# Stick-breaking attention by parts: the scan sums weights, the values become differences, gated outputs wait in DRAM

## The chip, the cores and the metric

The kernel runs on one core of one Trainium2 chip. The metric is the device time of one execution in microseconds. Kernels are compared by runs on the same chip. A profile of one execution, with a trace of every instruction, stands beside the times.

The engines in the profile are TensorE (PE; its weight loads are PEld), VectorE (DVE), ScalarE (ACT), GpSimd (POOL) and SyncE (SP), which issues the DMAs.

## The reference

Two layers, 1024 tokens, width 1024. Each layer projects the normalised input once, runs four groups of heads beside one another, normalises and gates each group's output, and projects back:

```
h = rmsnorm(x, g_pre) @ w_in
A: sliding-window attention   B: short gated convolution
C: latent attention           D: stick-breaking attention
y = concat(rmsnorm(out_g)) * silu(gate)
x = x + rmsnorm(y @ w_out, g_post)
```

The change is in group D (4 heads of 64):

```
z = q @ k.T * scale                       # per block of 128 queries, strictly causal
log_keep = where(mask, log_sigmoid(-z), 0)
after = cumsum(log_keep, reverse=True) - log_keep
a = where(mask, exp(log_sigmoid(z) + after), 0)
out = a @ v
```

So the weight of key j is its break probability times the product of the keep probabilities of all later keys.

## The kernel before, in words

All matrix products are done in three terms of a high and a low part (`split`: ScalarE casts the high part, VectorE subtracts it to get the low one), so TensorE has much work, and every operand passes ScalarE and VectorE once.

**Streams and planner.** The program is written as streams (Python generators): `gemm` (projections), `scores`, `pvs` (products with the values), `norms`, `z_parts` (splitting the gated outputs for the last projection), `w_out_rows`, `outs`, weight loading and others. `Weaver.run` steps through them and always takes the first stream in its list whose next piece is ready by its own clock; `gemm` is last in the list, so it fills TensorE where the others wait. `Weaver.enter` books each instruction on its engine with a cost from a formula, `Weaver.dma` books each transfer at 355 GB/s with fixed latencies around it (0.7 and 0.6 us ahead of the data, about 0.9 us behind it, 1.22 us from a ScalarE result to the issue), and the order that comes of these bookings is the order that each engine gets. On the chip an engine works through its list in that order and waits where something is late. All DMAs are issued by SP, in order.

**Tiles.** Most results live in 34 tiles `g` of 4 KB per partition: 16 hold the transposed input, 8 the outputs `y` of the four groups (two halves Q of 512 tokens), the others queries, keys, values and weights. Weight matrices `P` of the attention rows have 6 tiles. Projections write to 2 banks (`w_bank`), scores to 3, transposes to 2, value products to 1.

**Group D.** `d_v` projects the values of one tile of 128 tokens at a time (24 matmuls of 256 columns), and ScalarE and VectorE split the bank straight into the value tiles `Vt`. `d_q` and `d_k` project queries and keys of a pair of heads. `d_scores` computes the scores of one head and two blocks of 128 queries, ScalarE makes two sigmoids, the keep probabilities `kt` and the break probabilities `bt`. VectorE multiplies `kt` up from the right with one scan and then multiplies `bt` with the shifted result. `pv_causal` transposes the result on TensorE, splits it, and multiplies it with `Vt`.

**Order of a layer.** Group C's columns, group B, then `d_v`, `d_q(0)`, `d_k(0)`, gate 2, `d_q(1)`, half of gate 1, `d_k(1)` once the scores of the first pair are done, the other half of gate 1, the projections of group A, gate 3, gate 0. Group B's output lies in DRAM (`yBd`) from its normalisation until just before its gate.

Of the kernel before, what the change touches and what calls it, by code (L numbers as in the profile page):

```python
# [12 lines left out]
F32 = mybir.dt.float32  # L13
# [8 lines left out]
P = 128  # L22
S = 1024
D = 1024
# [69 lines left out]
class Weaver:  # L94
# [7 lines left out]
    def __init__(self, tc):  # L102
        self.tc = tc
        self.now = 0.0
        self.busy = {k: [] for k in "AVGDH"}
        self.acc = {}
        self.touched = {}
        self.opened = {}
        self.slots = {}
        self.banks = set()  # L110
        self.read = {}
        self.table = None
        self.users = []
        self.load_at = 0.0
        self.start = 0.0
        self.gone = set()
        self.last, self.tag = {}, {}
        self.funcs = [(0.0, 0)]
        self.port = {"V": [], "G": []}
        self.done = set()  # L120

    def alloc(self, ap, tag, bufs):
# [43 lines left out]
    def after(self, key, a, kinds):  # L166

        p0, p1, lo, hi = self.area(a)
        name = a.tensor.name
        t = self.opened.get(name, 0.0)  # L170
        if name not in self.acc:
            t = max(t, self.last.get(self.tag.get(name), 0.0))
        for (q0, q1, l, h, kind, k), end in self.acc.get(name, {}).items():
            if kind in kinds and q0 < p1 and p0 < q1 and l < hi and lo < h:
                t = max(t, end + LAT.get(k + key, 0.0))
        return t

    def ready(self, key, aps):
        return max([self.after(key, a, "w") for a in aps], default=0.0)
# [68 lines left out]
    def enter(self, key, op, args, kw):  # L248
        aps = [a for a in list(args) + list(kw.values()) if isinstance(a, bass.AP)]
        out = aps[0]  # L250
        outs = [out]
        if "accum_out" in kw:
            outs.append(kw["accum_out"])
        if op == "tensor_tensor_reduce":
            outs.append(aps[-1])
        n = 1
        for d in (aps[1] if op == "tensor_reduce" else out).shape[1:]:
            n *= d
        t = max(self.ready(key, aps[1:]), max(self.after(key, a, "rw") for a in outs))
        read = [a.tensor.name for a in aps[1:] if a.tensor.name in self.banks]  # L260
        bank = bool(read)
        for nm in read:
            for k, end in self.read.get(nm, {}).items():
                t = max(t, end + (LAT[k + key] if k != key else 0.0))
        scalars = sum(
            isinstance(args[i], bass.AP) for i in SCALARS.get(op, ()) if i < len(args)
        )
        func = args[2] if op == "activation" else None
        pair = False
        half = out.shape[0] <= 64 and n >= 128  # L270
        if key == "A":
            dur = (52.0 if bank else 93.0) + 0.833 * n
            dur += 93.5 * sum(isinstance(kw.get(k), bass.AP) for k in ("scale", "bias", "accum_out"))
            dur += 125.0 * half
            if func in TABLES and func:
                t = max(t, self.load_at)
        elif key == "V":
            fast = op == "tensor_scalar" and not bank
            dur = 69.0 + (0.52 if fast else 1.04) * n + 62.0 * scalars + 95.0 * half
            pair = (fast or op == "tensor_tensor") and not bank and n >= 128  # L280
            if op == "tensor_tensor_scan":
                dur = 110.0 + 2.12 * n
                pair = True
            elif op == "tensor_reduce":
                dur += 117.0
        elif op == "affine_select":
            dur = 244.0
        elif op == "memset":
            dur = 36.0 + 0.83 * n
        elif op == "tensor_scalar":  # L290
            dur = 244.0 + 0.833 * n
        else:
            dur = 148.0 + 2.25 * n
            pair = n >= 128
            if args[-1] == ALU.pow:
                dur = 400.0 + 162.0 * n
                pair = False
        t = self.place(key, t, dur, pair=pair)
        if key == "A" and func in TABLES and func:
            self.funcs = self.funcs[-60:] + [(t, func)]  # L300
        self.tc.cur_priority = int(t)
        for nm in read:
            self.read.setdefault(nm, {})[key] = t + dur
        by = "S" if op in ("tensor_tensor_scan", "tensor_tensor_reduce") else key
        for a in outs:
            self.note(by, a, "w", t + dur, t)
        for a in aps[1:]:
            self.note(key, a, "r", t + dur)
        return t
# [78 lines left out]
def tile_hybrid_trunk(  # L388
# [317 lines left out]
    def w_tiles():  # L706
# [11 lines left out]
        for L in LS:  # L718
# [11 lines left out]
                    chunk(L, f"B{key}{m}", c0 + m * P, P)  # L730
            chunk(L, "DV", O_DV, 256, True)
            for key in (
                "DQ0", "DK0", "G20", "G21", "DQ1", "G10", "DK1", "G11", "AV0", "AQ0", "AK0", "AQ1",
                "G30", "G31", "G00", "G01",
            ):
                if key[0] == "G":
                    c0 = O_G + 256 * int(key[1])
                else:
                    c0 = dict(DQ=O_DQ, DK=O_DK, AK=O_AK, AV=O_AV, AQ=O_AQ)[key[:2]]
                chunk(L, key, c0 + int(key[2]) * P, P, key == "G01")  # L740
# [412 lines left out]


    def group_b(L):
        l, yd = L["l"], L["yBd"]
        for m in range(2):
            us = [ftile(516), ftile(516)]

# [35 lines left out]
        A.activation(dst, pb, AF.Tanh, scale=0.5)  # L1195
        V.scalar_tensor_tensor(dst, dst, 1.0, pb, ALU.add, ALU.mult)

    def gate(L, grp, ms=(0, 1)):
        def ev(Q, pb):
            t = ftile()  # L1200
            silu(t, pb)
            z = L["y"][grp][Q]
            G.tensor_tensor(z[:, m, :], z[:, m, :], t, ALU.mult)
            W.release(t)

        for m in ms:
            yield from chunk_T(L, f"G{grp}{m}", ev)

    def gate_by_half(L):
# [12 lines left out]


    def d_v(L):
        yield room(4)
        Vt = [[gtile([P, 4, 2, P]) for _ in range(2)] for _ in range(NQ)]
        L["dV"] = Vt
        for t in range(NT):
            pb = w_bank()
            yield from mm3_w(L, "DV", pb[:, 0:256], "r", xtok(L["xt"], t), 2)  # L1230
            src = pb[:, 0:256].rearrange("p (m h d) -> p m h d", m=2, h=2)
            dst = [Vt[t // 4][hp][:, t % 4] for hp in range(2)]
            for hp in range(2):
                A.copy(dst[hp][:, :, 0:64], src[:, hp])
            for hp in range(2):
                V.tensor_tensor(
                    dst[hp][:, :, 64:128], src[:, hp], f(dst[hp][:, :, 0:64]), ALU.subtract
                )
            W.release(pb)
        done_with(L["W", "DV"])  # L1240

    def d_q(L, hp):
# [16 lines left out]
    def d_scores(L, hp, t0, hh):  # L1259
# [3 lines left out]
        for t in (t0, t0 + 1):  # L1263
# [6 lines left out]
            for o in range(0, w, cut):  # L1270
# [8 lines left out]
                A.activation(kt[:, o : o + n], sc[:, :n], AF.Sigmoid, scale=-0.125)  # L1279
                A.activation(bt[:, o : o + n], sc[:, :n], AF.Sigmoid, scale=0.125)  # L1280
                W.release(sc)
            rev = kt[:, w - 1 :: -1]
            V.tensor_tensor_scan(rev, rev, rev, 1.0, ALU.mult, ALU.bypass)
            V.tensor_tensor(bt[:, 0 : w - 1], bt[:, 0 : w - 1], kt[:, 1:w], ALU.mult)
            W.release(kt)
            Ps.append(bt)
        L["tasks"].append(
# [215 lines left out]
    ZORDER = (4, 5, 2, 3, 6, 7, 0, 1)  # L1503

    def z_split(L, grp, Q, wait=True):
        z = L["y"][grp][Q]
        free = W.idle_from("V")
        ts = []
        for m in range(2):
            if wait:  # L1510
                yield lambda: (ts or W.room("g", 2, 34)) and max(0.0, free() - 4000.0)
            ts = ts or [gtile([P, 2, 512]) for _ in range(2)]
            t = ts[m]
            split(t[:, 0, :], t[:, 1, :], z[:, m, :])
# [66 lines left out]
    for l in range(depth):  # L1581
        LS.append(
            dict(
                l=l, w=w_in[l], last=l == depth - 1, tasks=[], y=[[None, None] for _ in range(4)],
                yBd=[dp.tile([P, 2, 512], F32, name=nm("yBd")) for _ in range(NQ)],
                xt=[None, None], zt=[[None] * NK for _ in range(NQ)],
                wo=[[None] * NK for _ in range(2)],
                ss=cp.tile([P, 4 * NT], F32, name=nm("ss")),
# [54 lines left out]
    def gemm():  # L1643
        for L in LS:
# [11 lines left out]
            yield need(("norm", l, 2, 1))  # L1656
            yield from gate(L, 2)
            yield from d_q(L, 1)
            yield need(("norm", l, 1, 1))
            yield from gate(L, 1, (0,))  # L1660
            yield need(("scores", l, "D0"))
            yield from d_k(L, 1)
            W.mark("D", l, 1)
            yield from gate(L, 1, (1,))
            yield from a_v(L)
            yield from a_q(L, 0)
            yield need(("scores", l, "D1"))
            yield from a_k(L)
            yield from a_q(L, 1)
            yield need(("pv", l, "D1", 1))  # L1670
            L["y"][0] = [gtile([P, 2, 512], F32) for _ in range(NQ)]
            W.mark("A", l)
            yield need(("norm", l, 3, 1))
# [123 lines left out]
    def norms():  # L1797
        for L in LS:
            l = L["l"]
            yield need(("B", l))  # L1800
            for Q in range(NQ):
                y = [ftile(), L["yB1"][Q]]
                dma(y[0], L["yBd"][Q][:, 0, :])
                yield W.when(y[0])
                yield from group_norm_cols(l, 1, y)
                for m in range(2):
                    dma(L["yBd"][Q][:, m, :], y[m])
                W.release(*y)
            for Q in range(NQ):
                yield from norm(L, 2, "C", Q)  # L1810
            yield need(("D", l, 0))
            for Q in range(NQ):
                yield room(1)
                L["y"][1][Q] = gtile([P, 2, 512], F32)
                dma(L["y"][1][Q], L["yBd"][Q])
                W.mark("norm", l, 1, Q)
            yield need(("scores", l, "D1"))
            for Q in range(NQ):
# [52 lines left out]
```

## Time and profile before

| | us |
|---|---|
| median of 3 runs (lowest to highest) | 1160.34 (1159.23 to 1161.73) |
| the profiled execution: its time | 1160.64 |
| its span, first to last instruction | 1158.8 |
| TensorE busy | 1133.3 |
| VectorE busy | 815.0 |
| ScalarE busy | 639.7 |
| POOL busy | 345.0 |

The profiled execution's granted TensorE clock is 0.998 of full speed. Line 85 of the kernel is the helper through which all VectorE, ScalarE and POOL instructions go, line 497 is that of the matmuls, line 501 that of the transposes and line 414 that of the DMAs, so instructions are told apart by the tiles that they write and read: `xP` is an attention row, `xsc` a score bank, `xtr` a transpose bank, `xw` a projection bank or a weight tile, `xg` one of the 34 tiles, `xPT` a transposed and split attention row. A group in the profile reads: line, engine, operation, out<-in, shapes, xcount | busy us, mean ns of one | idle us before them and what ended it.

Stages in layer 0: the value projection of group D runs from 197 to 229 us, `d_q(0)` and `d_k(0)` to 251 us, group D's scores and products from 255 to 405 us, group A to about 495 us. Layer 1 has the same stages from 769, 799, 825 and 975 us on.

### The profile page before, as it was taken

Reading aid. Unit: us, or ns where it says so; the run is one execution under the profiler, and the core shown is the slowest. Engines: PE = TensorE matmul, PEld = TensorE weight load, DVE = VectorE, ACT = ScalarE, POOL = GpSimd, SP = SyncE. Lnnn points to the kernel's source line nnn. Section 1 sums busy time; section 2 is a strip of 40 time slices with the busy share of each in tenths; the row PEclk is TensorE's granted clock in tenths of the full one; section 3 lists DMA queues with packets and bytes.
Section 4 is the critical chain, followed back from the end, with each engine's and each line's share of the span. In section 5 each row is a group of like instructions: output and inputs, shape, how many; then the busy total and the mean of one; then the engine's idle time right before and its main releaser. Section 6 shows DMA issues by size and latency. Waiting matters only on the chain. (4 is left out here: it accounts for less than half of the span.)

```text
span 1158.8 us, 17859 instructions
## 1 busy us (share of the span) xinstructions
PE 1133.3 (98%) x6302; PEld 978.0 (84%) x6302; DVE 815.0 (70%) x1682; ACT 639.7 (55%) x1443; POOL 345.0 (30%) x480
## 2 busy tenths in 40 slices
PE   8999999999999999999999999999999999999997
PEld 6988889988888788878889888899888787887886
DVE  6868788549868988842764677874697789887324
ACT  7666566246656667632554655652664566875211
POOL 3215144114324244210231352530342333531000
PEclk9999999999999999999999999999999999999999
DMA  6120312121011012311450121121201101114123
GB/s 224 42 64 29 83 26 58 46 74 37 19 46 28 19 38 72 107 46 62 150 173 20 38 68 42 38 64 38 82 19 38 37 19 37 29 55 164 55 77 123
DMA packets 72677, 71.97 MB, mean 62 GB/s; under 512 B 10062, under 2 KB 59276, under 8 KB 72588
## 3 DMA queue, kind: packets, MB, share of 16 engines
q1 hardware_dynamic: 72588, 70.83, 20.6%
q8 instruction: 50, 0.82, 0.3%
q14 instruction: 39, 0.32, 0.1%
HBM read 55.09 MB, written 11.53 MB: 57 GB/s over the span
## 5 line engine op out<-in xcount | busy, mean ns | idle before, releaser
L497 PE MATMUL xw<-xg,xw 128*128 128x512 f32 x2064 | 516.8, 396 | 3.5 <-DVE xf L85 2.7
L497 PEld LDWEIGHTS xw<-xg,xw 128*128 128x128 f32 x2064 | 376.4, 188 | 78.1 <-DVE xf L85 4.4
L497 PE MATMUL xsc<-xg,xg 128*128 128x512 f32 (+7 forms) x1400 | 304.4, 363 | 0.4 <-DVE xs L85 0.4
L497 PEld LDWEIGHTS xsc<-xg,xg 128*128 128x128 f32 (+1 forms) x1400 | 238.9, 190 | 35.4 <-DVE xs L85 1.6
L85 POOL TENSOR_SCALAR xP<-xP,xs 128x256 f32<-128x256 f32 (+7 forms) x128 | 81.9, 652 | 169.7 <-DVE xs L85 77.7
L85 ACT CAST xPT<-xtr 128x512 fp32r<-128x512 f32 (+1 forms) x192 | 100.5, 553 | 56.4 <-PE xtr L501 54.9
L501 PE MATMUL xtr<-ident,xP 128*128 128x128 f32 (+1 forms) x843 | 122.5, 273 | 5.6 <-DVE xP L85 4.9
L85 DVE TENSOR_TENSOR xPT<-xtr,xPT 128x512 fp32r<-128x512 f32 (+1 forms) x192 | 116.3, 629 | 13.1 <-ACT xPT L85 12.6
L497 PE MATMUL xw<-xg,xg 128*128 128x416 f32 (+2 forms) x648 | 116.8, 327 | 0.2 <-DVE xg L85 0.2
L497 PE MATMUL xpv<-xPT,xg 128*128 128x256 f32 (+1 forms) x720 | 114.9, 286 | 0.4 <-DVE xPT L85 0.3
L497 PEld LDWEIGHTS xpv<-xPT,xg 128*128 128x128 f32 x720 | 102.9, 189 | 10.6 <-DVE xPT L85 1.9
L501 PEld LDWEIGHTS xtr<-ident,xP 128*128 128x128 f32 (+1 forms) x843 | 97.4, 140 | 16.0 <-DVE xP L85 6.7
L85 POOL TENSOR_TENSOR xw<-xraw,xw 128x512 fp32r<-128x512 f32 x47 | 68.4, 1458 | 138.9 <-ACT xw L85 106.5
L85 DVE TENSOR_TENSOR xg<-xw,xg 64x512 fp32r<-64x512 f32 (+1 forms) x112 | 62.8, 573 | 62.4 <-ACT xg L85 61.2
L85 ACT CAST xg<-xw 64x512 fp32r<-64x512 f32 (+1 forms) x112 | 53.6, 493 | 93.2 <-PE xw L497 81.6
L85 ACT ACTIVATE xP<-xP,xs 128x256 f32<-128x256 f32 (+7 forms) x128 | 80.7, 631 | 43.7 <-DVE xs L85 40.3
L497 PEld LDWEIGHTS xw<-xg,xg 128*128 128x128 f32 x648 | 102.1, 189 | 2.7 <-DVE xg L85 0.4
L85 DVE TENSOR_TENSOR_SCAN xP<-xP 128x128 f32<-128x128 f32 (+3 forms) x64 | 90.5, 1414 | 3.0 <-ACT xP L85 2.7
L85 POOL TENSOR_TENSOR xt<-xt 64x128 f32<-64x128 f32 x64 | 41.6, 650 | 146.5 <-DVE xt L85 131.6
L85 ACT ACTIVATE xP<-xsc 128x512 f32<-128x512 f32 (+2 forms) x192 | 79.7, 514 | 6.6 <-DVE xP L85 6.0
L85 ACT ACTIVATE xt<-xsc 128x512 f32<-128x512 f32 x32 | 19.1, 598 | 113.2 <-PE xsc L497 89.3
L85 ACT COPY xt<-xpv 64x512 f32<-64x512 f32 x80 | 46.7, 584 | 53.5 <-PE xpv L497 52.4
(129 smaller groups left out, 1284.5 us busy)
## 6 DMA issues: line engine op xcount, KB each, us to landing
xraw<-in_w_in_dram SPq DMA_DIRECT2D x96, 256.0 KB, 2.8
xP<-in_w_out_dram SPq DMA_DIRECT2D x16, 512.0 KB, 4.3
xg<-in_x_dram SPq DMA_DIRECT2D x8, 512.0 KB, 8.6
xg<-xP SPq DMA_DIRECT2D x32, 128.0 KB, 2.4
xP<-in_x_dram SPq DMA_DIRECT2D x8, 512.0 KB, 4.1
xP<-xs SPq DMA_DIRECT2D x8, 512.0 KB, 3.8
xs<-xP SPq DMA_DIRECT2D x7, 512.0 KB, 3.6
out_dram<-xP SPq DMA_DIRECT2D x7, 512.0 KB, 2.6
```

The lines of the kernel that those rows point to most:

```text
L85: ins = real(*args, **kw)
L497: in_order(T.matmul(ps, lhs, rhs, start=start, stop=stop, skip_group_check=True))
L501: in_order(T.transpose(ps, src, idn))
```

## The change

The weight of key j is the difference of two neighbouring values of a running sum: with S_j = kt_j * S_(j+1) + bt_j from the right, the weight of key j is S_j - S_(j+1), and summing by parts gives out = sum of S_j * (v_j - v_(j-1)). So `d_scores` leaves S from one scan, without the multiplication behind it, and `d_v` makes differences of neighbouring tokens' values. Tokens lie on partitions, so the value of the token before is one partition away; `differ` fetches it by DMA within SBUF, once for each half of 512 tokens.

Beside it: the outputs of groups 1 (B) and 2 (C) are written to DRAM after their gates and read back in `z_split`; `d_k(1)` comes ahead of gate 1 and no longer waits for the scores of the first pair; the output tiles of group A wait for room instead of the end of group D's products; and the planner's cost formulas are changed (`held`: a longer time where an operand starts in another group of 32 partitions than that of the instruction before; more operations count as using the port that VectorE and POOL share).

```diff
     def enter(...):
-        half = out.shape[0] <= 64 and n >= 128
+        half = self.held(key, out, aps[1:])
...
-            pair = (fast or op == "tensor_tensor") and not bank and n >= 128
+            pair = not bank and n >= 128 and op != "memset"
...
         elif op == "tensor_scalar":
             dur = 244.0 + 0.833 * n
+            pair = n >= 128
...
-    def gate(L, grp, ms=(0, 1)):
+    def gate(L, grp):
...
             G.tensor_tensor(z[:, m, :], z[:, m, :], t, ALU.mult)
             W.release(t)
+            if m and grp in L["yd"]:
+                dma(L["yd"][grp][Q], z)
+                W.release(z)
...
     def d_v(L):
         yield room(4)
         Vt = [[gtile([P, 4, 2, P]) for _ in range(2)] for _ in range(NQ)]
         L["dV"] = Vt
+        vs = []
+
+        def differ(Q):
+            u = gtile([P, 4, 256], F32)
+            if Q == 0:
+                V.memset(u[0:1, 0, :], 0.0)
+            else:
+                dma(u[0:1, 0, :], vs[0][127:128, 3, :])
+                W.release(vs[0])
+            dma(u[1:128], vs[Q][0:127])
+            dma(u[0:1, 1:4, :], vs[Q][127:128, 0:3, :])
+            V.tensor_tensor(u, vs[Q], u, ALU.subtract)
+            src = u.rearrange("p t (m h d) -> p m t h d", m=2, h=2)
+            for hp in range(2):
+                A.copy(Vt[Q][hp][:, :, :, 0:64], src[:, hp])
+            for hp in range(2):
+                V.tensor_tensor(
+                    Vt[Q][hp][:, :, :, 64:128], src[:, hp], f(Vt[Q][hp][:, :, :, 0:64]),
+                    ALU.subtract,
+                )
+            W.release(u)
+
         for t in range(NT):
+            Q, i = divmod(t, 4)
+            if i == 0:
+                yield room(1)
+                vs.append(gtile([P, 4, 256], F32))
             pb = w_bank()
             yield from mm3_w(L, "DV", pb[:, 0:256], "r", xtok(L["xt"], t), 2)
-            src = pb[:, 0:256].rearrange("p (m h d) -> p m h d", m=2, h=2)
-            dst = [Vt[t // 4][hp][:, t % 4] for hp in range(2)]
-            for hp in range(2):
-                A.copy(dst[hp][:, :, 0:64], src[:, hp])
-            for hp in range(2):
-                V.tensor_tensor(
-                    dst[hp][:, :, 64:128], src[:, hp], f(dst[hp][:, :, 0:64]), ALU.subtract
-                )
+            A.copy(vs[Q][:, i, :], pb[:, 0:256])
             W.release(pb)
+            if t in (4, 7):
+                yield room(1)
+                differ(t // 7)
+        W.release(vs[1])
...
     def d_scores(L, hp, t0, hh):
...
-            rev = kt[:, w - 1 :: -1]
-            V.tensor_tensor_scan(rev, rev, rev, 1.0, ALU.mult, ALU.bypass)
-            V.tensor_tensor(bt[:, 0 : w - 1], bt[:, 0 : w - 1], kt[:, 1:w], ALU.mult)
+            rev = bt[:, w - 1 :: -1]
+            V.tensor_tensor_scan(rev, kt[:, w - 1 :: -1], rev, 0.0, ALU.mult, ALU.add)
             W.release(kt)
...
     def z_split(L, grp, Q, wait=True):
+        back = grp in L["yd"]
+        if back:
+            yield room(3)
+            L["y"][grp][Q] = gtile([P, 2, 512], F32)
+            dma(L["y"][grp][Q], L["yd"][grp][Q])
+        z = L["y"][grp][Q]
...
     def gemm():
...
             yield from d_q(L, 1)
-            yield need(("norm", l, 1, 1))
-            yield from gate(L, 1, (0,))
-            yield need(("scores", l, "D0"))
             yield from d_k(L, 1)
             W.mark("D", l, 1)
-            yield from gate(L, 1, (1,))
+            yield need(("norm", l, 1, 1))
+            yield from gate(L, 1)
...
-            yield need(("pv", l, "D1", 1))
+            yield room(2)
             L["y"][0] = [gtile([P, 2, 512], F32) for _ in range(NQ)]
```

More of the change, by code (lines that the diff above doesn't have):

```diff
@@ L119, in __init__ @@
         self.port = {"V": [], "G": []}
+        self.rows = {}
         self.done = set()
@@ L176, in after, with held @@
         return t
+    def held(self, key, out, ins):
+        res = False
+        for kind, aps in (("r", ins), ("w", [out])):
+            for a in aps:
+                k = key, kind, a.tensor.name in self.banks
+                p0 = self.area(a)[0] // 32
+                res = res or self.rows.get(k, p0) != p0
+        for kind, aps in (("r", ins), ("w", [out])):
+            for a in aps:
+                self.rows[key, kind, a.tensor.name in self.banks] = self.area(a)[0] // 32
+        return res
     def ready(self, key, aps):
@@ L732, in w_tiles @@
             for key in (
-                "DQ0", "DK0", "G20", "G21", "DQ1", "G10", "DK1", "G11", "AV0", "AQ0", "AK0", "AQ1",
+                "DQ0", "DK0", "G20", "G21", "DQ1", "DK1", "G10", "G11", "AV0", "AQ0", "AK0", "AQ1",
                 "G30", "G31", "G00", "G01",
@@ L1155, in group_b @@
     def group_b(L):
-        l, yd = L["l"], L["yBd"]
+        l, yd = L["l"], L["yd"][1]
         for m in range(2):
@@ L1204, in ev @@
             W.release(t)
-        for m in ms:
+            if m and grp in L["yd"]:
+                dma(L["yd"][grp][Q], z)
+                W.release(z)
+        for m in range(2):
             yield from chunk_T(L, f"G{grp}{m}", ev)
@@ L1505, in z_split @@
     def z_split(L, grp, Q, wait=True):
-        z = L["y"][grp][Q]
         free = W.idle_from("V")
         ts = []
+        back = grp in L["yd"]
[4 more added lines that the diff above has]
+        z = L["y"][grp][Q]
         for m in range(2):
             if wait:
-                yield lambda: (ts or W.room("g", 2, 34)) and max(0.0, free() - 4000.0)
+                yield lambda: (ts or W.room("g", 2, 34)) and max(
+                    0.0, free() - 4000.0, W.ready("A", [z]) if back else 0.0
+                )
             ts = ts or [gtile([P, 2, 512]) for _ in range(2)]
@@ L1584, in tile_hybrid_trunk @@
                 l=l, w=w_in[l], last=l == depth - 1, tasks=[], y=[[None, None] for _ in range(4)],
-                yBd=[dp.tile([P, 2, 512], F32, name=nm("yBd")) for _ in range(NQ)],
+                yd={g: [dp.tile([P, 2, 512], F32, name=nm("yd")) for _ in range(NQ)] for g in (1, 2)},
                 xt=[None, None], zt=[[None] * NK for _ in range(NQ)],
@@ L1802, in norms @@
                 y = [ftile(), L["yB1"][Q]]
-                dma(y[0], L["yBd"][Q][:, 0, :])
+                dma(y[0], L["yd"][1][Q][:, 0, :])
                 yield W.when(y[0])
@@ L1806, in norms @@
                 for m in range(2):
-                    dma(L["yBd"][Q][:, m, :], y[m])
+                    dma(L["yd"][1][Q][:, m, :], y[m])
                 W.release(*y)
@@ L1810, in norms @@
                 yield from norm(L, 2, "C", Q)
-            yield need(("D", l, 0))
+            yield need(("D", l, 1))
             for Q in range(NQ):
@@ L1814, in norms @@
                 L["y"][1][Q] = gtile([P, 2, 512], F32)
-                dma(L["y"][1][Q], L["yBd"][Q])
+                dma(L["y"][1][Q], L["yd"][1][Q])
                 W.mark("norm", l, 1, Q)
```

## The prediction, made before the changed kernel was run

> **What bounds the kernel now.** I read the page's busy shares first, then busy time by stage, then who ended TensorE's waits, then the costliest VectorE groups.
>
> ```profile
> PE 1133.3 (98%) x6302; PEld 978.0 (84%) x6302; DVE 815.0 (70%) x1682; ACT 639.7 (55%) x1443; POOL 345.0 (30%) x480
> ```
>
> TensorE is busy in 1133.3 of 1158.8 us, so at most 25.5 us of visible idle time can be won anywhere, and the change touches no matmul. The profiled execution took 1160.64 us, its span 1158.8; the median of the runs is 1160.34. My sum is made against 1160.6. Where the idle time lies, by stage (busy us of PE, PEld, DVE, ACT, POOL; then clock, DMA share, GB/s):
>
> ```profile
> 197.00:229.00 32.00, 32.00 (x272) 31.87 (x271) 20.80 (x47) 11.92 (x32) 6.19 (x8) 1.00 0.17 51
> 799.00:820.00 21.00, 21.00 (x96) 17.45 (x95) 6.21 (x9) 6.60 (x12) 2.52 (x2) 1.00 0.26 82
> 255.00:405.00 150.00, 145.57 (x799) 121.20 (x798) 127.29 (x164) 92.57 (x197) 53.30 (x48) 1.00 0.12 30
> 825.00:975.00 150.00, 145.56 (x800) 121.22 (x799) 127.22 (x165) 92.56 (x197) 53.30 (x48) 1.00 0.11 29
> 405.00:500.00 95.00, 92.67 (x528) 79.18 (x527) 77.64 (x185) 66.37 (x162) 36.10 (x51) 1.00 0.26 80
> 1120.00:1140.00 20.00, 20.00 (x90) 16.57 (x89) 9.30 (x20) 2.76 (x8) 2.18 (x4) 1.00 0.43 157
> ```
>
> The two stick-breaking stages (255 to 405 and 825 to 975) have VectorE at 127 of 150 us and TensorE idle 4.4 us in each. The value projection of that group (197 to 229 in layer 0) has no TensorE idle at all: it is plain projection work. TensorE's own waits name VectorE:
>
> ```profile
> PE xtr L501 <- DVE xP L85: 4.9, 3, 2.3
> PE xw L497 <- DVE xf L85: 2.7, 4, 0.9
> ```
>
> The longest, 2.3 us, is a transpose waiting for a finished weight tile `P`. So VectorE late in the stick-breaking stage is a real cost, and a small one: 8.9 us in both layers.
>
> **The change, part by part.** *The multiplication behind each scan goes.*
>
> ```profile
> L85 DVE TENSOR_TENSOR xP<-xP,xP 128x127 f32<-128x127 f32 (+3 forms) x64 | 60.0, 937 | 6.0
> L85 DVE TENSOR_TENSOR_SCAN xP<-xP 128x1024 f32<-128x1024 f32 x8 | 18.7, 2343 | 0.0
> L85 DVE TENSOR_TENSOR_SCAN xP<-xP 128x128 f32<-128x128 f32 x8 | 4.2, 528 | 0.4 <-ACT xP L85 0.4
> ```
>
> 64 instructions and 60.0 us leave VectorE, 30 us per stage: 127 becomes about 97 of 150 us, and each chain from scores to transposes is shorter by about 0.9 us. The scan stays one instruction with two inputs; (2343-528)/896 is 2.03 ns per element now. Adding instead of bypassing in its second step could cost nothing (my value: same instruction, same element count) or, at worst, half as much again per element: 64 scans of 576 elements on average at 1 ns are 37 us, still below the 60 removed. So VectorE gains 23 to 60 us, and what TensorE can get is its 8.9 us of idle in the two stages. I take 7.0 us off; the ends are 0 and 15, the latter if nearly as much waiting hides inside matmuls counted as busy.
>
> *The scores of heads 2 and 3 may start sooner* (their keys are projected ahead of the gate, and the sliding-window scores no longer wait for the last products). That moves matmuls and removes none; a stage with TensorE at 97% has room only for the same 8.9 us, so it is counted inside the 7. The changed costs of the planner reorder all stages a little: 0, with ends of -4 and +4 (the idle of 405 to 500 is 2.3 us per layer).
>
> *The value projection.* Now each of eight token tiles is cast and subtracted straight out of the bank:
>
> ```profile
> L85 DVE TENSOR_TENSOR xg<-xw,xg 128x128 fp32r<-128x128 f32 x32 | 7.8, 283 | 9.4 <-ACT xg L85 9.2
> L85 ACT CAST xg<-xw 128x128 fp32r<-128x128 f32 x32 | 6.9, 269 | 27.5 <-PE xw L497 27.3
> L85 ACT CAST xg<-xg 128x512 fp32r<-128x512 f32 x32 | 19.0, 624 | 7.4 <-DVE xg L85 7.4
> L85 DVE TENSOR_TENSOR xP<-xP,xP 128x1023 f32<-128x1023 f32 x8 | 11.4, 1427 | 0.8
> ```
>
> These 64 go. In come per layer eight ScalarE copies of 256 elements (about 0.4 each, as two casts of 128 overlap to 0.43 below), four casts of 512 (0.62), and on VectorE two differences of 1024 (1.2 without POOL beside it, 1.4 by the row) and four subtractions of 512 (0.7). Both engines stay within 5 us of what they did in both layers, in a stretch where they are 65% and 37% busy. As busy time this costs nothing.
>
> What it adds to the path is a **wait**: `differ` fetches the value of the token before by a DMA from SBUF to SBUF, `u[1:128] <- vs[Q][0:127]`, 127 rows of 4 KB, 520,192 bytes, once per half and layer, four times in all. VectorE's subtraction waits for it, then ScalarE's two casts wait for VectorE, each at its place in a fixed order. The planner books it at 355 GB/s: 1.5 us of data, about 4.9 us from the last copy to the subtraction. What do transfers cost here?
>
> ```profile
> q1 hardware_dynamic: 72588, 70.83, 20.6%
> xg<-xP SPq DMA_DIRECT2D x32, 128.0 KB, 2.4
> xP<-xs SPq DMA_DIRECT2D x8, 512.0 KB, 3.8
> xg<-xyBd SPq DMA_DIRECT2D x4, 512.0 KB, 4.2
> ```
>
> The 512 KB rows (3.8 and 4.2 us) have 128 partitions, and the SBUF-to-SBUF row (2.4 us) has 32: both divide into 16 equal shares for 16 DMA engines. 127 is prime: equal shares exist for one engine alone. That is the question of this change, and no row answers it. If it is spread, it costs about 4 us and is hidden. If one engine moves all of it, its price comes from the share columns: 157 GB/s at a share of 0.43 is 157/(0.43 x 16) = 22.8 GB/s per engine, and over the whole span 70.83 MB in 20.6% of 16 x 1158.8 us is 18.5. So 22.8 to 28.1 us of data. The fixed part is 2.0 (2.4 less the 0.4 that 8 KB per engine take). Landing after 24.8 us, or 30.1 by the slower rate; I take 24.8, the rate of a stretch with large rows. I choose one engine, because a division into equal shares is what every row-wise transfer of this trace allows, and a scheme without it would have to be seen first.
>
> [...]
>
> What stands behind that wait, from layer 0 (TensorE, then ScalarE, then VectorE, in order of time):
>
> ```profile
> 222.51 0.87 PE L497 MATMUL xw<-xw,xg 128*128 128x256 f32 x6
> 223.22 2.32 PE L497 MATMUL xw<-xg,xg 128*128 128x256 f32 x18
> 225.38 0.88 PE L497 MATMUL xw<-xw,xg 128*128 128x256 f32 x6
> 226.10 2.32 PE L497 MATMUL xw<-xg,xg 128*128 128x256 f32 x18
> 228.26 11.98 PE L497 MATMUL xw<-xg,xw 128*128 128x512 f32 x52
> 215.66 0.43 ACT L85 CAST xg<-xw 128x128 fp32r<-128x128 f32 x2 [2.06 <-PE xw L497]
> 219.40 0.43 ACT L85 CAST xg<-xw 128x128 fp32r<-128x128 f32 x2 [3.31 <-PE xw L497]
> 222.71 0.43 ACT L85 CAST xg<-xw 128x128 fp32r<-128x128 f32 x2 [2.88 <-PE xw L497]
> 225.58 0.43 ACT L85 CAST xg<-xw 128x128 fp32r<-128x128 f32 x2 [2.44 <-PE xw L497]
> 235.13 1.39 DVE L85 TENSOR_TENSOR xg<-xw,xg 64x512 fp32r<-64x512 f32 x2 [5.72 <-ACT xg L85]
> ```
>
> The casts at 215.66, 219.40, 222.71 and 225.58 belong to tiles 3 to 6. *First half:* `vs[0]` is full at 216.1. The difference is planned at 221, its casts at about 222.3, so the copy of tile 5 (ready at 222.7) stands behind them on ScalarE. TensorE has two banks: it finishes tile 6 at 225.5 and stops. The rows land at 216.1 + 24.8 = 240.9; difference 1.2, two casts 1.3, the copy 0.4: TensorE goes on at 243.8. Stall 18.3 us. *Second half:* tile 7 takes 2.9 us (24 matmuls, 225.38 to 228.26), to 246.7; its copy ends at 247.1, the rows land at 271.9, the difference ends at 273.1, then VectorE's two subtractions of the first query half (1.39, as at 235.13) end at 274.5 and free a bank. TensorE had two query halves of 24 matmuls to do, at 21.00/96 = 0.22 us 10.5 to 10.9 us in all, to 257.6. Stall 16.9 us. Per layer 35.2, in both 70.4 us. Nothing else can fill it: all remaining streams need VectorE or ScalarE, and weight casts stand behind the same wait.
>
> *Outputs parked in DRAM.* Gates 1 and 2 write eight tiles of 512 KB and read eight (four reads replace those of before). SP waits for POOL's product before each write and holds weight loads behind it; two raw buffers are ahead and the DMA share is 0.26 there. A reload lands in 4.2 us by its row, and the casts it feeds come some 15 us or more ahead of the output projection. I take 0; at the worst one reload per layer is late, +8.4 us.
>
> Sum: 1160.6 - 7.0 + 70.4 = 1224.0.
>
> **The rivals.**
> *Rival 1, the shift is spread evenly enough:* it lands in about 4 us as booked, and the kernel is faster: 1160.6 - 7.0 = 1154, between 1146 and 1158. For it: all 512 KB rows land in 3.8 to 4.2 us. Against it: all of them have row counts divisible by 16. It decides when the landing is below 4.9 + 4.5 us, the slack that the second bank leaves in the first half.
> *Rival 2, one engine, with other transfers behind it:* weight loads use all 16 engines, so a sixteenth of each queues behind the 127 rows; where the slower rate (18.5 GB/s) holds, each stall grows by 5.3 us, and a late weight tile adds a few more: 1224 + 21 = 1245, up to 1262. It is the upper part of my forecast's range.
> *Rival 3, spread, and the freed VectorE time buys nothing,* since weights, ScalarE and the two banks set the pace in the stick-breaking stages: 1160.6, within 2 us; with a late reload up to 1169.
>
> **How the numbers follow.** One engine (forecast and rival 2): 0.84, of it 0.25 for rival 2. Rival 1: 0.12. Rival 3: 0.04, half of it slower. A difference under 0.2% (2.3 us) can't be told from no change. So faster 0.12, same 0.02, slower 0.86. Range: the low end is 1176 (a gain of 15, and each stall 10 us shorter, half by a transfer faster than these rows show and half by more work in front of it), the high end 1262. That leaves the spread cases out.
>
> **What would show it.** Right: the row of `xg<-xg` transfers of 508 KB lands in over 20 us; VectorE's longest waits name that DMA, four times some 20 us; TensorE has four gaps of 15 to 20 us, two in each value projection, with a DMA share near 1/16; the group of 64 multiplications is gone, scans keep 2.0 ns per element, and TensorE's idle in the stick-breaking stages falls to 1 or 2 us. Wrong: a landing near 4 us, or gaps that other work fills; a scan that takes 3 ns per element; or new gaps at the end of a layer that name the reload.

## The result and the profile after

| | before | changed |
|---|---|---|
| median, us (lowest to highest) | 1160.69 (1159.23 to 1161.73) | 1215.57 (1215.08 to 1215.72) |
| span of the profiled execution | 1158.8 | 1213.8 |
| TensorE busy / idle in the span | 1133.3 / 25.5 | 1138.6 / 75.2 |

The changed kernel is slower by a factor of 1.0473 (95% interval 1.0455 to 1.0491), 55 us. One of the ten executions of experiment 6 ran at a granted clock of 0.557 and took 1877.82 us; the ratio given there is made without it. The page's first part, of the changed kernel (busy us, share of the span, instructions), and its chain of work that ended last:

```profile
PE 1138.6 (94%) x6302; PEld 984.4 (81%) x6302; DVE 761.9 (63%) x1606; ACT 641.6 (53%) x1435; POOL 341.6 (28%) x474
PE 80%; DMA 7%; ACT 4%; DVE 4%; issue 2%; POOL 1%; SPq 0%; DVEq 0%; POOLq 0%; ACTq 0%
```

TensorE executes the same 6302 matmuls and transposes, VectorE has 53 us less to do, and a DMA is now 7% of the chain. Three of the waits, those for the shift and TensorE's two largest (us in total, times, longest):

```profile
DVE xg L85 <- DMA xg<-xg: 79.7, 4, 24.3
PE xw L513 <- DVE xg L85: 34.9, 4, 17.1
PE xw L513 <- ACT xg L85: 27.0, 2, 13.6
```

Four waits of VectorE for the shift, and TensorE behind them, 62 us in six waits; 61 us of it are four gaps, two in each layer. The order in time in layer 0: SP's issues, VectorE's differences, ScalarE's copy of tile 5 and the casts of the first difference, and TensorE's two gaps.

```profile
215.66 26.44 SPq L430 DMA_DIRECT2D xg<-xg  x4
243.34 0.67 SPq L430 DMA_DIRECT2D xg<-xg  x1
238.91 1.23 DVE L85 TENSOR_TENSOR xg<-xg,xg 128x1024 f32<-128x1024 f32 x1 [15.91 <-DMA xg<-xg]
267.09 1.23 DVE L85 TENSOR_TENSOR xg<-xg,xg 128x1024 f32<-128x1024 f32 x1 [24.27 <-DMA xg<-xg]
222.31 0.37 ACT L85 COPY xg<-xw 128x256 f32<-128x256 f32 x1 [2.94 <-PE xw L513]
240.17 1.14 ACT L85 CAST xg<-xg 128x512 fp32r<-128x512 f32 x2 [17.49 <-DVE xg L85]
241.63 13.43 PE L513 MATMUL xw<-xg,xw 128*128 128x512 f32 x48 [13.61 <-ACT xg L85]
272.13 13.54 PE L513 MATMUL xw<-xg,xw 128*128 128x512 f32 x48 [17.07 <-DVE xg L85]
```

The first of SP's four issues from 215.66 on is the shift of the first half (26.44 us run to the end of the fourth). The shift issued at 215.66 lets VectorE go at 238.91, the one of 243.34 at 267.09: 23.3 and 23.8 us. Stretches of the same time (busy us of PE, PEld, DVE, ACT, POOL; clock, DMA share, GB/s):

```profile
228.00:241.00 13.00, 0.01 (x1) 0.00 (x0) 1.41 (x2) 0.83 (x2) 0.00 (x0) 0.69 0.05 20
241.60:245.00 3.40, 3.37 (x8) 2.70 (x9) 1.21 (x2) 0.77 (x2) 0.00 (x0) 0.50 0.30 67
246.00:255.00 9.00, 9.00 (x39) 7.09 (x37) 0.00 (x0) 0.00 (x0) 0.00 (x0) 0.97 0.06 23
290.00:440.00 150.00, 149.95 (x844) 127.01 (x843) 110.26 (x154) 97.44 (x206) 52.07 (x49) 1.00 0.18 51
```

While TensorE stands still from 228 to 241, DMAs are busy for a share of 0.05 (of the page's 16 engines 0.8), at 20 GB/s. The packets (one for each row of 4 KB) say the same. The DMA view from 216 to 239 us:

```profile
DMA packets 193, 0.54 MB, mean 24 GB/s; under 512 B 65, under 2 KB 65, under 8 KB 192
```

127 packets are between 2 and 8 KB (192 less 65). In the trace they run one after another: the first starts at 216.98, most follow 0.156 us behind the one before, and the last ends at 238.15. Behind the gap TensorE runs at a clock of 0.50 for 4.8 us, from 241.63 to 246.47. And the stick-breaking stage (290 to 440) has no idle time left: 0.05 us in 150, where it had 4.4.

### The profile page after: what moved, and what is told of

It is laid out like the page before. It is cut to its first block, busy times and chain, and to the rows that moved or that the text cites. A ratio compares the mean times of both kernels' runs of the same rounds, so it can differ in the third digit from the quotient of the medians.

```text
span 1213.8 us, 17788 instructions
## 1 busy us (share of the span) xinstructions
PE 1138.6 (94%) x6302; PEld 984.4 (81%) x6302; DVE 761.9 (63%) x1606; ACT 641.6 (53%) x1435; POOL 341.6 (28%) x474
## 4 chain that ended last, share of the span: by engine, by line
PE 80%; DMA 7%; ACT 4%; DVE 4%; issue 2%; POOL 1%; SPq 0%; DVEq 0%; POOLq 0%; ACTq 0%
PE xw L513 41%; PE xsc L513 23%; PE xtr L517 9%; DMA xg<-xg 7%; PE xpv L513 7%; ACT xP L85 2%; DVE xP L85 1%; DVE xg L85 1%; ACT xg L85 1%; DVE xs L85 1%; POOL xs L85 0%; DVE xt L85 0%; PE xsc L517 0%; ACT xt L85 0%; POOL xP L85 0%
## 5 line engine op out<-in xcount | busy, mean ns | idle before, releaser
L513 PE MATMUL xw<-xg,xw 128*128 128x512 f32 x2064 | 524.3, 401 | 61.2 <-DVE xg L85 34.2
L513 PEld LDWEIGHTS xw<-xg,xw 128*128 128x128 f32 x2064 | 382.7, 191 | 138.3 <-issue 35.7
L513 PE MATMUL xsc<-xg,xg 128*128 128x512 f32 (+7 forms) x1400 | 301.1, 361 | 0.0
L85 POOL TENSOR_TENSOR xw<-xraw,xw 128x512 fp32r<-128x512 f32 x37 | 50.4, 1361 | 201.2 <-ACT xw L85 179.3
L85 DVE TENSOR_TENSOR_SCAN xP<-xP,xP 128x128 f32<-128x128 f32 (+3 forms) x64 | 89.3, 1413 | 10.1 <-ACT xP L85 9.3
L85 DVE TENSOR_TENSOR xg<-xw,xg 64x512 fp32r<-64x512 f32 x80 | 55.1, 689 | 58.3 <-ACT xg L85 57.7
L85 DVE TENSOR_TENSOR xg<-xg,xg 128x512 fp32r<-128x512 f32 (+3 forms) x56 | 38.7, 721 | 83.1 <-DMA xg<-xg 79.7
L85 POOL TENSOR_TENSOR xt<-xt 64x128 f32<-64x128 f32 x64 | 48.3, 755 | 128.4 <-DVE xt L85 116.2
L85 ACT CAST xg<-xw 64x512 fp32r<-64x512 f32 x80 | 46.6, 582 | 59.3 <-PE xw L513 46.9
```

The costliest lines, as they stand in the source:

```text
L85: ins = real(*args, **kw)
L513: in_order(T.matmul(ps, lhs, rhs, start=start, stop=stop, skip_group_check=True))
```

## The experiments

**1. The shift in two pieces, 112 and 15 rows.**

```diff
-            dma(u[1:128], vs[Q][0:127])
+            dma(u[1:113], vs[Q][0:112])
+            dma(u[113:128], vs[Q][112:127])
```

> The changed kernel with the shift of 127 rows as two transfers, 112 rows and 15 rows. Theory (equal shares, so 127 rows go through one DMA engine): 112 rows are 7 for each of 16 engines and 15 rows one for each of 15, both land in under 4 us, the four gaps of TensorE (61 us) and the half-clock stretches behind them (about 9 us) vanish: 1145 us, between 1140 and 1151. Rival 1 (a copy that moves every row to the next partition is slow as such): still two gaps per layer, 1210 us or more. Rival 2 (VectorE's place in the order, not the landing, makes the gaps): 1205 us or more.

Measured: 1145.26 us (1144.20 to 1145.52), ratio to before 0.9868 (0.9849 to 0.9888). SP's issue of the second half's pieces and VectorE's difference:

```profile
228.21 1.45 SPq L430 DMA_DIRECT2D xg<-xg  x2
232.26 1.23 DVE L85 TENSOR_TENSOR xg<-xg,xg 128x1024 f32<-128x1024 f32 x1 [5.27 <-DMA xg<-xg]
```

Both pieces are there 4.0 us after the issue, and no wait of TensorE for VectorE's results in the value projection is longer than 0.5 us. Here the 127 packets of 4 KB run side by side, from 229.40 to 231.71. The same bytes, moved to the same partitions, cost 70.3 us less (1215.57 to 1145.26).

**2. 125 and 2 rows. 3. 113 and 14 rows.** The same line with other cuts.

> The changed kernel with the shift as 125 rows and 2 rows. Equal shares: 125 rows are 25 for each of 5 engines, a fifth of 127 in one: about 4.2 us of data, landing in 6 to 7 us, hidden but for at most 1 us per transfer: 1145 to 1150 us. Rival (an odd row count, or one that does not fill whole groups of partitions, falls back to one engine): landing in over 20 us and 1212 us.

> The changed kernel with the shift as 113 rows (a prime) and 14 rows. Equal shares: 113 rows in one engine, 113/127 of 21 us of data, so each of the four gaps is about 2.3 us shorter: 1206 us, between 1202 and 1210. Rival (it is 127, the last partition or the rows' total that matters, so a smaller piece is spread): 1145 us.

Measured: 1151.33 us (ratio 0.992, 0.9894 to 0.9946) and 1207.30 us (ratio 1.0402, 1.0375 to 1.043). With 125 rows, the issue and VectorE's difference in the second half:

```profile
229.50 1.54 SPq L430 DMA_DIRECT2D xg<-xg  x2
236.96 1.23 DVE L85 TENSOR_TENSOR xg<-xg,xg 128x1024 f32<-128x1024 f32 x1 [8.67 <-DMA xg<-xg]
```

With 113 rows, the same for the first half:

```profile
215.28 24.50 SPq L430 DMA_DIRECT2D xg<-xg  x5
236.59 1.23 DVE L85 TENSOR_TENSOR xg<-xg,xg 128x1024 f32<-128x1024 f32 x1 [13.96 <-DMA xg<-xg]
```

The rows are there 7.5 us after the issue with 125 rows, 21.3 with 113, 23.3 with 127. A piece with an odd count, a shift by one partition and a tile not filled by one transfer are common to all three cuts; what differs is the largest divisor up to 16 of the larger piece: 16 for 112 rows (4.0 us), 5 for 125 (7.5), 1 for 113 and 127 (21 to 24). Equal shares, one for each engine used, fit all four landings, and none of the rivals does; the trace does not name the engine of a packet. 125 rows came out 1.3 us above the upper end of what was expected: the landing is later by 0.5 us or more, TensorE waits 2.0 us once per layer, and in layer 1 its clock halves behind that wait (last section).

**4. Matmuls in the gaps.** In the changed kernel, 58 matmuls on unused data behind tile 7 and 75 ahead of `d_k(0)`, written to a transpose bank and read by nobody.

> The changed kernel with matmuls that nobody reads, 58 and 75 of 512 bf16 columns, at the place of the two gaps in each layer. The gaps stay as long as the transfer makes them, but TensorE has work in them. Theory (half the granted clock after a gap is a price of its own, about 2.3 us a gap): granted clock 1.0 behind the gaps and 1206 us, between 1203 and 1209. Rival (what follows a gap is slow because operands come late, not for the clock): 1215 us within 3.

Measured: 1213.99 us (ratio to before 1.0457, 1.0439 to 1.0475): 1.6 us less than the changed kernel, not 9. Layer 1, the 48 matmuls behind each gap, in the changed kernel and then here:

```profile
840.06 12.90 PE L513 MATMUL xw<-xg,xw 128*128 128x512 f32 x48 [13.43 <-ACT xg L85]
870.08 13.22 PE L513 MATMUL xw<-xg,xw 128*128 128x512 f32 x48 [17.12 <-DVE xg L85]
```

```profile
838.67 11.21 PE L513 MATMUL xw<-xg,xw 128*128 128x512 f32 x48 [1.11 <-ACT xg L85]
869.00 12.61 PE L513 MATMUL xw<-xg,xw 128*128 128x512 f32 x48 [2.92 <-DVE xg L85]
```

The half clock is real: 48 matmuls take 11.2 us when TensorE was kept busy and 12.9 to 13.2 behind a gap. So the time lies in the range of the rival, but its cause, late operands, is not what the rows show. The time behind the first gap is not lost twice: the second transfer starts from tile 7's copy, not from these matmuls, so a faster TensorE waits longer in the second gap. Only the second gap's price reaches the end, and in layer 1 the 2.9 us that the extra matmuls left idle halved the clock again. From the last value matmuls to the first score, layer 1 takes 58.8 us in both kernels, so the 1.6 us were won in layer 0. My expectation had added up four prices where two count.

**5. A copy of 127 rows for which nobody waits. 6. The same copy in two pieces.** In the kernel before, behind `d_v`'s splits of tiles 4 and 7 (`dp` is the pool of DRAM tiles):

```diff
+            if t in (4, 7):
+                cpy = dp.tile([P, 4, 2, P], F32, name=nm("cpy"))
+                dma(cpy[1:128], f(Vt[t // 7][0][0:127]))
```

> The kernel before, with a copy of 127 rows of 4 KB from each half of the value tiles to DRAM behind the value projection, for which nobody waits (four in all, as many as the changed kernel's shifts). Theory (the wait of VectorE and ScalarE is the cost, not the busy DMA engine): 1160.7 us within 4, the copy landing in about 22 us, weight transfers issued beside it landing late by up to that much. Rival (weight transfers behind it stall TensorE too): 1175 us or more.

> The kernel before with the copy to DRAM that nobody waits for, as 112 rows and 15 rows instead of 127. By the theory that one DMA engine's queue holds up the weights, the copies cost nothing: 1160.5 us within 3. If it is the extra bytes or the extra place in SP's order, 1175 us or more as with one transfer of 127 rows.

Measured: 1182.16 us (ratio 1.0178, 1.0164 to 1.0192) for the one piece, 1161.91 us (ratio 1.0, 0.9989 to 1.001) for 112 and 15 rows. My theory that only the wait costs was wrong; the rival holds. With one piece, the transfers of 225 to 262 us, what ScalarE and TensorE waited for, and TensorE's 12 matmuls ahead of its gap:

```profile
xraw<-in_w_in_dram SPq DMA_DIRECT2D x3, 256.0 KB, 22.0
251.87 3.01 PE L497 MATMUL xw<-xg,xw 128*128 128x512 f32 x12
261.07 0.62 ACT L85 CAST xw<-xraw 128x512 fp32r<-128x512 f32 x1 [11.53 <-DMA xraw<-in_w_in_dram]
261.74 5.99 PE L497 MATMUL xw<-xg,xw 128*128 128x512 f32 x12 [6.87 <-ACT xw L85]
```

A weight load of 256 KB, which otherwise lands in 2.8 us, takes 22.0 when issued at 238.96 behind the second copy, which itself stood behind the first. In the trace, 480 of the load's 512 packets run from 246.9 to 248.5, and its last 32, one share of 16, only after 259.8, as the second copy ends. (SP needs 7.3 us instead of 0.4 to issue this load; why was not tried.) TensorE stands still for 6.9 us in each layer, and behind that gap 12 matmuls of the same shape take 6.0 us instead of 3.0: the clock is halved there too (0.74 on the mean from 250 to 270 us). So the transfer that had its rows one after another held up one share of 16 of the load issued behind it, and four such copies cost 21 us in all; as 112 and 15 rows the same copies cost nothing (1161.91 us).

**7. The parts alone. 8. All but the parts. 9. All with the old formulas.** From the kernel before, the new `d_v` (112 and 15 rows) and the new scan; from experiment 1, the old `d_v`, scan and multiplication; from experiment 1, the old cost formulas.

> The kernel before with the values' differences (shift of 112 and 15 rows) and the scan by parts alone: no outputs in DRAM beyond those of before, old order, old planner costs. Theory (less VectorE work is what the attention stages gain from): most of the gain, 1148 us, between 1144 and 1153. Rival (the earlier start of the scores of heads 2 and 3 and of group A is the gain): 1158 us or more.

> The changed kernel with the old value projection and the old scan and multiplication: outputs in DRAM, new order and new planner costs alone. By the theory that VectorE's work is the gain, 1157 us, between 1152 and 1162; by the rival that the new order is, 1148 us or less.

> The changed kernel with the shift of 112 and 15 rows and the old cost formulas of the planner. The new formulas are worth little: 1145 us, between 1142 and 1149; if the order that they give carries the gain, 1152 us or more.

**10. The formulas alone. 11. The order and the outputs in DRAM alone. 12. Parts and formulas.** The same pieces, combined the other way.

> The kernel before with the planner's new cost formulas alone; no work is changed, only the order that the planner makes. If the order of streams and the outputs in DRAM carry what the rest of the change gains, 1160 us within 3; if the new formulas do, 1150 us or less.

> The kernel before with the outputs of groups 1 and 2 in DRAM and the new order of projections and of group A's start, old cost formulas, old value projection, old scan and multiplication. If the earlier start of the scores gives TensorE work in its gaps, 1149 us, between 1146 and 1152; if the new formulas carry it, 1158 us or more.

> The kernel before with the values' differences (shift of 112 and 15 rows), the scan by parts and the planner's new cost formulas; old order of projections, no further outputs in DRAM. If the gain of the formulas alone (3 us) is one that emptied gaps have already given, 1143.7 us within 1.5, as without them; if it is separate, 1141 us.

| parts | order, DRAM | formulas | us | ratio to before (95%) |
|---|---|---|---|---|
| yes | | | 1143.68 | 0.9849 (0.9836 to 0.9863) |
| | yes | | 1148.22 | 0.9889 (0.9873 to 0.9905) |
| | | yes | 1157.64 | 0.9971 (0.9958 to 0.9984) |
| | yes | yes | 1148.24 | 0.9887 (0.9873 to 0.9900) |
| yes | yes | | 1144.73 | 0.9856 (0.9843 to 0.9870) |
| yes | | yes | 1143.08 | 0.9843 (0.9824 to 0.9863) |
| yes | yes | yes | 1145.26 | 0.9868 (0.9849 to 0.9888) |

The parts are worth 17 us by themselves (1143.68 us, 0.3 below the range expected), the order with the outputs in DRAM 13, and together they are worth no more than the parts alone. I had expected the rest alone at 1157 us; it came to 1148, as its rival said. Both fill the same gaps. The stick-breaking stage with the parts alone, and then with the order alone:

```profile
255.00:405.00 150.00, 150.00 (x843) 126.98 (x843) 108.50 (x153) 97.82 (x206) 53.50 (x50) 1.00 0.12 30
```

```profile
255.00:405.00 150.00, 148.72 (x833) 125.48 (x832) 129.96 (x175) 97.29 (x205) 52.89 (x52) 1.00 0.18 52
```

With the order alone VectorE is as busy as before, 130 of 150 us, and TensorE's idle time still falls from 4.4 to 1.3 us. That other products are ready while a chain is late is the likely reason; the waits were not followed one by one. With the parts the chain is shorter, VectorE is at 108.5 and the idle time is 0. In the stage behind it (405 to 500 us) the same holds: TensorE's idle time is 2.3 us before, 0.02 with the parts and 0.8 with the order. The formulas alone gain 3 us, and nothing where the gaps are empty already: with the parts they make 1143.08 of 1143.68. Of the longer times that they book, the trace of the kernel before shows that beside POOL: of VectorE's eight multiplications of 511 elements four take 0.69 us with POOL idle and four 1.53 us beside one of its TENSOR_TENSORs. That a shared port is the cause, and the longer time for another group of 32 partitions, are the planner's assumptions; no run shows them. The parts alone, and the parts with the formulas, are the fastest, 1.5% below the kernel before, and both beat the changed one; their intervals do not tell them apart.

## Why the prediction was right

*One engine.* The step that decided the sign was that 127 rows have no equal shares, which no row of before showed. The transfer took 23.3 and 23.8 us to its reader (24.8 forecast), its data 21.2 us (22.8 forecast), and the cuts of experiments 1 to 3 show the dependence on the divisor, with landings at 4.0, 7.5, 21.3 and 23.3 us. The low end of the range had each landing some 5 us earlier by a faster transfer; no run shows one, the 127 rows were 1.0 to 1.5 us faster than forecast.

*The price, 70.4 us forecast.* Measured as the difference to the same kernel with the shift in two pieces, 70.3 us. The total is right, and its pieces are not. In the changed kernel (layer 1) and then with two pieces, from the last value matmuls to the first score:

```profile
824.31 2.32 PE L513 MATMUL xw<-xg,xg 128*128 128x256 f32 x18
883.14 0.34 PE L513 MATMUL xsc<-xg,xg 128*128 128x128 f32 x2
```

```profile
788.19 2.32 PE L513 MATMUL xw<-xg,xg 128*128 128x256 f32 x18
790.35 21.95 PE L513 MATMUL xw<-xg,xw 128*128 128x512 f32 x96
812.13 0.34 PE L513 MATMUL xsc<-xg,xg 128*128 128x128 f32 x2
```

58.8 against 23.9 us, 34.9 per layer (35.2 forecast). Of it the first gap is 13.4 (18.3 forecast), the second 17.1 (16.9), and the 96 matmuls take 26.1 instead of 21.95, 4.2 us of half clock that the forecast did not have. The first gap was too long in the forecast for two reasons, each worth some 2 us. I put the copy of tile 5 behind the casts of `differ`; in fact it stood ahead of them (222.31 against 240.17 in the ScalarE rows above), so TensorE did tile 7 before the gap and stopped at 228.0, not at 225.5. And TensorE went on at 241.6, not at 243.8, since the rows were there at 238.9, not at 240.9. The second gap agrees only as a sum: in layer 0 the half clock kept TensorE busy 2.5 us longer ahead of it (13.4 against 10.9), and from the rows' landing to TensorE's next matmul it was 5.0 us (267.09 to 272.13), not 2.6. That such errors cancel to 0.1 us of 70 is luck; that two stalls per layer behind the landing make the price is not.

*The gain, 7.0 us forecast.* Measured 15.3 (1160.54 to 1145.26, experiment 1). This is the mis-sized term, 0.3 us beyond its end of 15. I counted 7 of the 8.9 us of visible idle time of the two stick-breaking stages and nothing of the stage behind each. By windows of equal length the first falls from 8.9 to 0.1 us, and the second from 5.0 to 1.6. In the whole span experiment 1 has 11.4 us less idle time (25.5 to 14.1) and 5.0 us less busy time (1133.3 to 1128.3) for the same 6302 instructions. Of these 5.0 us, 1.9 are half clock: in the profile of the kernel before, one wait of 2.2 us is followed by it (a mean clock of 0.83 from 1060 to 1070 us), and experiment 1 has no such stretch.

```profile
1060.54 2.90 PE L497 MATMUL xsc<-xg,xg 128*128 128x512 f32 x12
1065.61 1.11 PE L501 MATMUL xtr<-ident,xt 128*128 128x128 f32 x4 [2.17 <-DVE xt L85]
1066.38 4.26 PE L497 MATMUL xsc<-xg,xg 128*128 128x512 f32 x12
1070.47 0.60 PE L501 MATMUL xtr<-ident,xs 128*128 128x128 f32 x4
```

Four transposes take 1.11 instead of 0.60 us, and 12 matmuls of one shape 4.26 instead of 2.90. What makes the other 3 us is not shown; waiting inside matmuls counted as busy, as the prediction put it for its upper end, is one reading. Sum 1160.6 - 15.3 + 70.3 = 1215.6; the forecast of 1224 was off by the gain.

*The scan* kept its price, with the addition in its second step: 89.3 us for 64 against 90.5 before.

```profile
L85 DVE TENSOR_TENSOR_SCAN xP<-xP,xP 128x128 f32<-128x128 f32 (+3 forms) x64 | 89.3, 1413 | 10.1 <-ACT xP L85 9.3
```

*Outputs in DRAM* were forecast at 0, at most 8.4. Taken with the order they gain 13 us by themselves; behind the parts the two together cost 1.0 to 2.2 us (1143.68 to 1144.73 without the formulas, 1143.08 to 1145.26 with them), at the edge of what these intervals resolve. What the outputs alone are worth without the order was not tried. The changed kernel makes 12 reloads of 512 KB, not the eight that I counted: the four of group B's output ahead of its gate stayed.

*Rival 1* had its bound too wide: by the slack of the first half a landing up to 9.4 us was to be harmless, and in experiment 2 one of 7.5 us already left TensorE waiting for 2.0 us in the second half of each layer. *Rival 2*, transfers queued behind the 127 rows, was not the changed kernel's cause (TensorE's waits name VectorE and ScalarE), but experiment 5 shows that it is real where VectorE does not wait first.

## What to carry to other kernels

Before adding a DMA whose row count is not a multiple of 16, look at its divisors: here 112 rows landed in 4.0 us, 125 in 7.5, 113 in 21.3 and 127 in 23.3, so this shift by one partition is 112 and 15 rows, not 127, and the difference was 70 us of 1160. The price of a slow transfer is not its share of DMA time but what stands behind its reader, and behind it in the queue, in an order that was planned for a fast one. And gains that empty the same gap are not added: shorter chains (17 us) and other work in the gap (13 us) made 15 to 16 together.

## What the runs showed of the hardware that was not expected

In the changed kernel the granted clock falls to 0.50 in gaps of 13 to 17 us, 3.5 to 5.1 us after TensorE stops, and stays there for 3.7 to 5.1 us after it goes on. Idle stretches of 2.2 us in the kernel before and of 2.9 us in experiment 4 were followed by the half clock too. In experiment 4 the same gap stands ahead of the same 48 matmuls in layer 0 and in layer 1:

```profile
272.00:277.00 5.00, 4.17 (x18) 3.49 (x19) 2.06 (x3) 1.71 (x3) 2.54 (x2) 1.00 0.35 81
868.00:873.00 5.00, 4.00 (x11) 3.23 (x12) 2.22 (x4) 1.85 (x4) 2.55 (x2) 0.66 0.33 68
272.83 11.14 PE L513 MATMUL xw<-xg,xw 128*128 128x512 f32 x48 [2.89 <-DVE xg L85]
```

The clock stayed full once (1.00, and the 48 matmuls take 11.14 us) and was halved once (0.66 on the mean of the stretch, 12.61 us in the rows of experiment 4). The traces show what differs. They hold each change of the clock, and within an execution all changes lie whole multiples of 3.41 us apart (3.41 us in the kernel before, from 1065.64 to 1069.05, 13.65 and 17.07 us in the changed kernel). On a grid of such steps, laid through the changes of each execution, the time that TensorE idles within one step sorts the short gaps:

| kernel | TensorE idle, us | most of it within one step, us | clock behind it |
|---|---|---|---|
| experiment 4, layer 0 | 269.94 to 272.83 | 1.50 | full |
| before | 389.06 to 391.39 | 1.59 | full |
| experiment 5, layer 1 | 980.86 to 983.18 | 1.83 | full |
| experiment 10 | 388.52 to 390.85 | 1.95 | half |
| experiment 2, layer 1 | 805.16 to 807.17 | 2.01 | half |
| before | 1063.45 to 1065.61 | 2.17 | half |
| experiment 4, layer 1 | 866.09 to 869.00 | 2.58 | half |

In all 14 traces, past the first 20 us of each, every step at full clock with 1.95 us or more of idle TensorE (15 steps) is followed by the half clock, and none with 1.83 us or less is. In the first 20 us three steps with 1.50 to 1.68 us of idle time were followed by it as well. So by these traces a gap of 2 to 3 us costs the clock or not by where it falls on the grid (full behind 2.3 us at 389.06 and half behind 2.2 us at 1063.45, in one execution of the kernel before). No run moved a gap on purpose to try this.
